# Attention block with 32 experts on one core: earlier bias selectors, a later change of slots, other places for raw rows and gates

## The chip, the core and the metric

The kernel runs on one core of a Trainium2 chip. TensorE (PE) multiplies, VectorE (DVE) and ScalarE (ACT) work on the results and prepare operands, GpSimd (POOL) and SyncE (SP) issue most of the loads. The metric is the device time of one execution in microseconds; before the change the median of three runs is 1178.18 us (1177.84 to 1178.41).

## The reference

One layer for 256 tokens of width 1024, all in fp32. A projection `w_in` feeds three attention branches (fox with a forget gate, dilated, and attention to a memory) and three gates. The branches are merged and projected, and a layer norm follows. A router picks 4 of 32 experts for each token, and a last layer norm ends the layer.

```python
merged = (gates[:, :, 0] * jnp.einsum('bse,ed->bsd', o_fox, w_br_fox[l])
          + gates[:, :, 1] * jnp.einsum('bse,ed->bsd', o_dil, w_br_dil[l])
          + gates[:, :, 2] * jnp.einsum('bse,ed->bsd', o_mem, w_br_mem[l]))
y = jnp.einsum('bsd,de->bse', merged, w_out[l])
h = layer_norm(DEEPNORM_ALPHA * h + y, ln1_g[l], ln1_b[l])
y_moe = moe_ffn(h.reshape(B * S, D), w_router[l], b_router[l], w_exp_in[l], b_exp_in[l], ...)
h = layer_norm(DEEPNORM_ALPHA * h + y_moe, ln2_g[l], ln2_b[l])
...
def expert_block(args):                      # in moe_ffn
    xe, e = args
    h = xe @ w1[e] + b1[e]
    return clamped_swiglu(h) @ w2[e] + b2[e]
```

The weights of one expert are a 1024 x 2048 and a 1024 x 1024 matrix, 12.58 MB; all 32 make 402 MB.

## The kernel before

**Attention.** Weights arrive in pieces. Each lands in one of four raw slots (w0 to w3), ACT casts it (`L212`, the high part), DVE subtracts the cast from the raw form (`L205`, the low part), and PE forms three products of high and low parts (`L225`, `product`). The split views lie in a ring of slots h4 to h7 and h2. `use()` runs before each step of PE and splits some steps ahead. The transposed tokens (`xT`) and the memory (`memT`) are the first operands; before the change their pieces go through the same four raw slots. `load_to(n)` issues a piece's DMA on SP. The matrices come in the order g0, kv, mq, fv, fq, fk, dq, dk, dv, g2, g4, br0, g1, g3, g5, br1, wo (g: gates, br: branch projections, wo: output projection).

**Rows of the biases.** `raw1` holds the rows of b1, `raw2` those of b2 and of the norms. `rows_of` (L641 to L649) splits them into high and low parts b1s, b2s and lnr. Before the change POOL loads them at the start, and they are split between the steps of the gates g1 and g3.

**Norm stage.** The output projection, the residual, the layer norm, router and top 4 are interleaved by hand (L790 to L862).

**Experts.** Each expert handles up to 64 tokens. `gather` picks its tokens with a product by a one-hot matrix, `inner` is the first matrix product (bias product L938, weights L945), `swiglu` follows, `outer` is the second product (L977, L983), and `scatter` (L993) adds to the accumulators. The order on PE is inner(e + 1), outer(e), gather, scatter(e). In experts 1 to 4 a `residual` adds a piece of the residual as well. The bias product multiplies b1s by `own`, a matrix that selects the rows of expert e; `choose(e)` makes it on DVE:

```python
own[e] = p2.tile([P, P], F32R, tag="own", name="own")
nc.vector.tensor_scalar_mul(own[e], c2[:, CBL:CUS], c2[:, CSUM + e:CSUM + e + 1])
```

**Order of the weight stream.** `unit` (L903 to L924) loads 2 MB of expert weights into the next of eleven small places of 16 KB a partition (`turn`; some consist of two half slots, each with its own DMA). From expert LARGE on it loads 4 MB into five places of 32 KB a partition (`turn2`), which lie over the small ones: a big slot can be loaded once the small units under it have been used. A place is loaded again when the products that read it have ended. SP issues in its written order, and a DMA whose place isn't free holds all behind it. The first eleven units are put among the attention's weight pieces (`issue_after`, EXPERTS_FROM).

PE, DVE and ACT run in the order in which the code is written (`manual_schedule`); SP and POOL are ordered by a scheduler.

Of the kernel before, what the change touches and what calls it, by code (L numbers as in the profile page):

```python
# [11 lines left out]
F32 = mybir.dt.float32  # L12
# [9 lines left out]
P = 128  # L22
# [6 lines left out]
C = 64  # L29
# [12 lines left out]
LARGE = 10  # L42
# [39 lines left out]
def block_kernel(ctx: ExitStack, tc: tile.TileContext, x, xT, memT, w_in, b_fgate, t5, w_mem_kv, w_br, w_out,  # L82
# [10 lines left out]
    EXPERTS = ("H01", "h4", "h5", "H67", "X", "O", "W", "h2", "h3", "M", "m", "e", "E")  # L93
# [34 lines left out]
    s = const.tile([P, 2, GB, C], F32, name="s")  # L128

# [10 lines left out]
    with ExitStack() as s1:  # L140
# [22 lines left out]
        plan, views, raw, marks, steps, n_load, n_part, n_ring, n_used = [], [], [], [], [], [0], [0, 0], [0], [0]  # L163
# [6 lines left out]
        def x_piece(src, v, k, n):  # L170
            plan.append((src[:, k:k + n], lambda: v[k // 4][:, :, k % 4:k % 4 + n]))

        def w_piece(src, where, k, n):

            i, f = len(plan), src.shape[-1]
# [11 lines left out]
            plan.append((src[:, k:k + n], take))  # L187
# [4 lines left out]
        def load_to(n):  # L192
            while n_load[0] < min(n, len(plan)):
                src = plan[n_load[0]][0]
                k, f = src.shape[1:]
                raw.append(slot(f"w{n_load[0] % 4}", k, f))
                marks.append(nc.sync.dma_start(raw[-1], src))
                n_load[0] += 1

        def split(a, b):  # L200

            while n_part[0] < a or n_part[1] < b:
                if n_part[1] < min(b, n_part[0]):
# [3 lines left out]
                    load_to(i + 5)  # L207
                else:
                    i = n_part[0]
                    load_to(i + 1)  # L210
# [17 lines left out]
        def cols(i, n=P):  # L228
            return slice(i * n, (i + 1) * n)
# [40 lines left out]
        mT, mv_ = halves("o")  # L270
        W = {}
# [20 lines left out]
        matrix("wo", w_out, n=1)  # L292

# [187 lines left out]
        nc.tensor.matmul(po[:, P:T], lf[1], NU[:, 0:P], start=False, stop=True)  # L481
        g = turned(xTs, W["fk"], 3, "ps_k")
        next(g)
        ckf = at.tile([P, T], F32, tag="o", name="ckf")
# [3 lines left out]
        next(g)  # L488

# [3 lines left out]
        next(g)  # L493
        ps = next(g)
        k_f = evict_qk(ps, 3, False, "k_f")

# [98 lines left out]
        gate2 = pg.tile([P, 4, T], F32, tag="gt2", name="gt2", bufs=1)  # L595
# [4 lines left out]
        pz = s6.enter_context(tc.tile_pool(name="pz", bufs=4, space=PSUM, **TILES))  # L600
# [11 lines left out]
        zeros = p3.tile([P, 512], BF16, name="zeros", bufs=1)  # L612
# [16 lines left out]

        raw1, raw2 = place(0, F32, "raw1"), place(1, F32, "raw2")  # L630
        nc.gpsimd.memset(raw2, 0.0)
        for g in range(2):
            for i in range(2):
                r = slice(64 * g + 32 * i, 64 * g + 32 * i + NE)
                nc.gpsimd.dma_start(raw1[r].rearrange("p (i f) -> p i f", i=2),
                                    b1.rearrange("e (i g f) -> e g i f", i=2, g=2)[:, g])
                nc.gpsimd.dma_start(raw2[r, 0:512], b2[:, cols(g, 512)])
        for i in range(2):
            nc.gpsimd.dma_start(raw2[32 * i:32 * i + 8, 512:1024], ln.rearrange("r (g f) -> (r g) f", g=2))

        def rows_of(i):  # L641

            src, dst, n = ((raw1, b1s.rearrange("p i f -> p (i f)"), 2), (raw2[:, 0:512], b2s, 2), (raw2[0:C, 512:1024], lnr, 1))[i // 2]
            if i % 2 == 0:
                nc.scalar.copy(dst, src)
            else:
                for g in range(n):
                    r = slice(64 * g + 32, 64 * g + 64)
                    nc.vector.tensor_sub(dst[r], src[r], dst[r].bitcast(F32))  # L649

        mg_t = []
        mgT = lambda u, k: mg_t[k // 4][:, u, k % 4].bitcast(F32R)
        for c in range(2):
            gates = [gate01[:, 0:4], gate01[:, 4:8], gate2] if c == 0 else []
            for b in range(len(gates), 3):
                for i, ps in enumerate(turned(xTs, W[f"g{2 * b + c}"], 4, "ps_g", new=bank2)):
                    if b < 2 and i % 2 == 0 or b == 1 and i % 2:
                        rows_of(i // 2 if b == 0 else 2 + i)
                g = pg.tile([P, 4, T], F32, tag=f"gt{b}", name=f"gt{b}", bufs=1) if b else slot("h3", 4, T)
# [21 lines left out]
        s6.close()  # L681
# [90 lines left out]
        def ahead(n):  # L772

            for i in range(n):
                nc.tensor.matmul(gx[i % 2], zeros[:, 0:P], zeros, start=True, stop=False)
# [13 lines left out]

        nc.scalar.activation(zT[0][:, 0, 0:1], mg_t[1][:, 0, 3, T - 1:T], AF.Sqrt, scale=0.0)  # L790
# [16 lines left out]
        normal(0, 0, nc.scalar)  # L807
        choice(0)
# [10 lines left out]
        normal(0, 1, nc.scalar)  # L819
        ahead(2)  # L820
        route(1, range(4, 6))
        turn_back(1, 6, 2)
# [49 lines left out]
    with ExitStack() as s1:  # L872
# [25 lines left out]
        turn = (("N",), ("H01",), ("h2", "e"), ("E",), ("X",), ("O",), ("W",), ("M",), ("h3", "h4"), ("H67",), ("h5", "m"))  # L898
# [4 lines left out]
        def unit(e, u, large, pieces=1, last=False):  # L903
# [14 lines left out]
            for c in [0, 2048, 4096, 6144, 7168] if last else range(0, w * len(names), n):  # L918
# [3 lines left out]
                with tc.issue_after(before.ins) if n_u[0] <= len(turn) else ExitStack():  # L922
                    loads.append(nc.sync.dma_start(at(c, n), src))
            return at  # L924

        own, own_last = {}, []

        def choose(e):

            own[e] = p2.tile([P, P], F32R, tag="own", name="own")  # L930
            nc.vector.tensor_scalar_mul(own[e], c2[:, CBL:CUS], c2[:, CSUM + e:CSUM + e + 1])  # L931
# [99 lines left out]
        with tc.manual_schedule(engines={PE, DVE, ACT}):  # L1031

            choose(0)
# [267 lines left out]
```

## Time and profile before

| | |
|---|---|
| median of 3 runs | 1178.18 us |
| profiled execution | 1178.88 us |
| its span | 1176.7 us |
| PE busy | 1104.2 us (94%) |
| DVE, ACT busy | 330.3 us (28%), 208.6 us (18%) |
| bytes moved | 443.90 MB, mean 377 GB/s |
| SP's queue | 36576 packets, 440.15 MB, 90.4% of 16 engines' span |

The span runs from the first to the last instruction on the core; the execution's time is 2.2 us longer. The busy share of PE is an average: it counts products that run at the slow clock, and products that only follow the arrival of weights. Which of the two, PE or the weight stream, is late at a place is read from the waits there. "Clock" is the granted clock of PE as a share of the full one (1.00 is 2.4 GHz, 0.50 is 1.2 GHz).

### The profile page before, as it was taken

The page shows a single profiled execution, that of the slowest core. Times are in us where ns is not written, and L with a number is a line of the kernel's source. Part 1 is how long each engine was busy: PE and PEld are TensorE (multiplying, and loading weights), DVE is VectorE, ACT ScalarE, POOL GpSimd, SP SyncE. Part 2 cuts the span into 40 slices and gives each one's busy share as a digit, 9 for nine tenths or more (in the row PEclk, how much of TensorE's full clock was granted, in tenths as well). Part 3 has the DMA queues.
Part 4 walks back from the last instruction along what each step waited for, and adds up shares of the span by engine and source line. Part 5 has one row for each costly group of instructions (what it writes and reads, how often), then busy time and mean ns, then how long its engine had stood idle before and what let it go on. Part 6 is the DMA issues. An engine that isn't in the chain of part 4 may idle for free.

```text
span 1176.7 us, 13733 instructions
## 1 busy us (share of the span) xinstructions
PE 1104.2 (94%) x5854; PEld 543.5 (46%) x5854; DVE 330.3 (28%) x662; ACT 208.6 (18%) x391; POOL 17.4 (1%) x36
## 2 busy tenths in 40 slices
PE   7999999979999999999999999999999998999996
PEld 6899899734333333333333333333333333333322
DVE  4656675622221212111111221111111111111113
ACT  4655544421000001000100100000000000000011
POOL 3000110000000000000000000000000000000000
PEclk8999999989999999999999999999999999999999
DMA  7964687879999999879999999999999999999992
GB/s 229 314 216 148 221 283 239 325 316 428 424 427 427 425 423 422 361 321 431 435 431 429 429 433 433 432 427 432 433 431 429 432 433 429 431 428 427 425 421 115
DMA packets 37745, 443.90 MB, mean 377 GB/s; under 512 B 4442, under 2 KB 4736, under 8 KB 17712
## 3 DMA queue, kind: packets, MB, share of 16 engines
q1 hardware_dynamic: 36576, 440.15, 90.4%
q0 software_dynamic: 1104, 2.82, 1.0%
q8 instruction: 48, 0.79, 0.3%
q14 instruction: 17, 0.14, 0.0%
HBM read 441.90 MB, written 1.06 MB: 376 GB/s over the span
## 4 chain that ended last, share of the span: by engine, by line
PE 49%; DMA 30%; DVE 5%; ACT 2%; issue 1%; DVEq 0%; ACTq 0%
PE h L945 22%; PE yp L983 13%; DMA slot_DC<-in_wx 11%; DMA slot_DB<-in_wx 7%; DMA slot_DD<-in_wx 6%; DMA slot_DA<-in_wx 3%; PE ps_x L886 3%; DMA slot_DF<-in_wx 3%; PE ps_g L225 2%; PE h L938 1%; PE ps_b L225 1%; PE y L225 1%; ACT xe L891 1%; PE ps_a L969 1%; DVE xe L893 1%; PE acc L993 1%
## 5 line engine op out<-in xcount | busy, mean ns | idle before, releaser
L1249 DVE TENSOR_SCALAR h<-h 128x512 f32<-128x512 f32 x32 | 22.4, 699 | 438.3 <-PE h L945 438.3
L962 ACT COPY sgT<-ps_s 128x256 f32<-128x256 f32 x32 | 11.9, 372 | 498.1 <-PE ps_s L960 498.1
L205 DVE TENSOR_TENSOR slot_h<-slot_w,slot_h 128x1024 fp32r<-128x1024 f32 (+3 forms) x73 | 78.5, 1089 | 33.5 <-ACT slot_h L212 33.2
L225 PE MATMUL ps_g<-slot_x,slot_h 128*128 128x256 f32 x576 | 74.4, 291 | 5.7 <-ACT slot_h L212 3.7
L212 ACT CAST slot_h<-slot_w 128x1024 fp32r<-128x1024 f32 (+3 forms) x73 | 68.1, 944 | 49.0 <-PE ps_g L225 8.8
L225 PEld LDWEIGHTS ps_g<-slot_x,slot_h 128*128 128x128 f32 x576 | 72.4, 198 | 7.8 <-ACT slot_h L212 4.8
L986 DVE COPY ys<-yp 128x512 f32<-128x512 f32 x31 | 21.4, 692 | 184.1 <-PE yp L983 184.1
L945 PE MATMUL h<-slot_DF,xe 128*64 128x512 f32 x288 | 63.9, 595 | 1.8 <-DMA slot_DF<-in_wx 1.8
L971 ACT COPY actT<-ps_a 128x512 f32<-128x512 f32 x32 | 18.7, 585 | 260.6 <-PE ps_a L969 260.6
L945 PE MATMUL h<-slot_DD,xe 128*64 128x512 f32 x288 | 63.6, 594 | 0.0
L945 PE MATMUL h<-slot_DC,xe 128*64 128x512 f32 x288 | 63.6, 594 | 0.0
L945 PE MATMUL h<-slot_DB,xe 128*64 128x512 f32 x288 | 63.5, 593 | 0.0
L993 PE MATMUL acc<-ys,sgT 64*128 64x512 f32 x248 | 61.6, 615 | 0.4 <-DVE ys L986 0.4
L886 PE MATMUL ps_x<-s,zn 128*128 128x128 f32 x480 | 58.3, 275 | 0.0
L945 PE MATMUL h<-slot_DA,xe 128*64 128x512 f32 x256 | 56.6, 594 | 0.1
L886 PEld LDWEIGHTS ps_x<-s,zn 128*128 128x128 f32 x480 | 55.9, 192 | 0.0
L893 DVE TENSOR_SCALAR xe<-ps_x,lnc 128x128 f32<-128x128 f32 x60 | 24.6, 410 | 79.0 <-ACT xe L891 79.0
L938 PE MATMUL h<-b1s,own 128*128 128x512 f32 x64 | 23.7, 453 | 23.4 <-DVE own L931 23.4
L983 PE MATMUL yp<-slot_DA,actT 128*64 128x512 f32 x160 | 37.4, 619 | 4.2 <-DMA slot_DA<-in_wx 4.2
L983 PE MATMUL yp<-slot_DC,actT 128*64 128x512 f32 x160 | 35.9, 597 | 5.4 <-DMA slot_DC<-in_wx 5.4
L945 PEld LDWEIGHTS h<-slot_DF,xe 128*64 128x64 f32 x288 | 20.1, 137 | 42.9 <-issue 38.0
L983 PE MATMUL yp<-slot_DD,actT 128*64 128x512 f32 x128 | 33.4, 683 | 6.0 <-DMA slot_DD<-in_wx 6.0
(316 smaller groups left out, 1260.2 us busy)
## 6 DMA issues: line engine op xcount, KB each, us to landing
slot_DC<-in_wx SPq DMA_DIRECT2D x12, 4096.0 KB, 38.5
slot_DB<-in_wx SPq DMA_DIRECT2D x12, 4096.0 KB, 39.2
slot_DA<-in_wx SPq DMA_DIRECT2D x11, 4096.0 KB, 38.8
slot_DD<-in_wx SPq DMA_DIRECT2D x11, 4096.0 KB, 38.5
slot_DF<-in_wx SPq DMA_DIRECT2D x11, 4096.0 KB, 39.4
slot_h<-in_wx SPq DMA_DIRECT2D x21, 1024.0 KB, 13.6
slot_H<-in_wx SPq DMA_DIRECT2D x10, 2048.0 KB, 13.9
slot_w<-in_w_in_g SPq DMA_DIRECT2D x23, 512.0 KB, 4.8
```

Source lines behind the costliest of these rows:

```text
L205: nc.vector.tensor_sub(views[i][:, 1].bitcast(F32R), raw[i], views[i][:, 0])
L212: nc.scalar.copy(views[i][:, 0].bitcast(F32R), raw[i])
L225: nc.tensor.matmul(ps, a(u, k)[:, ca], b(v, k)[:, cb], start=first and i + j == 0, stop=last and i == 2 and j == len(ks) - 1)
L886: nc.tensor.matmul(ps[:, i * GB * C:(i + 1) * GB * C], zn[tt][:, (c + i) * P:(c + i + 1) * P], s[:, tt].rearrange("p a b -> p (a b)"), sta ...
L893: nc.vector.tensor_scalar(t[:, c + i, :], ps[:, i * GB * C:(i + 1) * GB * C], g, b_, op0=ALU.mult, op1=ALU.add)
L938: nc.tensor.matmul(hp[i], own[e], b1s[:, i], start=True, stop=False)
L945: nc.tensor.matmul(hp[i][g * C:(g + 1) * C, :], xt[:, k, s0:s0 + C], wt(k % n * 2 * FF + i * FF + g * 512, 512), start=False, stop=k == KD ...
L971: nc.scalar.copy(actT, ps.rearrange("p (a b) -> p a b", a=4))
L983: nc.tensor.matmul(yp[g * C:(g + 1) * C, :], actT(k), wt(k % n * D + g * 512, 512), start=False, stop=k == KD - 1)
L986: nc.vector.tensor_copy(ys, yp)
L993: nc.tensor.matmul(acc[tt][g], sgT[r, tt * P:(tt + 1) * P], ys[r, :], start=e == 0, stop=False)
L1249: nc.vector.tensor_scalar_min(hg, hg, LIMIT)
```

## The change

- `choose` moves to the constants with three buffers. It makes the selectors of experts 0 and 1 before the norm stage, that of 2 in expert 0, and afterwards each one an expert ahead, behind `swiglu`.
- LARGE goes from 10 to 12: 70 small units instead of 58, then 61 big ones.
- The raw form of the tokens and the memory has a slot of its own (N), and `load` counts only the weight pieces against the four raw slots.
- The raw rows of biases and norms are loaded by SP behind a weight piece of the middle of the attention, and split among the fk products.
- The gates gt1 and gt2 lie in the buffers of `xe`, gt0 in the place of zn0; gates and branch products stay in the banks of pool `pp`, which closes later.
- (h3, f) is the fifth place of the turn, and the order and the layout of the small places are new. E is the fourth in both.
- In the norm stage `normal(0, 1)`, `turn_back(1, 6, 2)` and `route(1, range(4, 6))` stand earlier, and the fillers of `ahead` read a smaller operand.

```diff
-LARGE = 10
+LARGE = 12
...
-    EXPERTS = ("H01", "h4", "h5", "H67", "X", "O", "W", "h2", "h3", "M", "m", "e", "E")
+    EXPERTS = ("H01", "h4", "h5", "H67", "X", "O", "W", "h2", "h3", "a", "b", "f", "e", "E")
...
+    def choose(e):
+        own[e] = const.tile([P, P], F32R, tag="own", name="own", bufs=3)
+        nc.vector.tensor_scalar_mul(own[e], c2[:, CBL:CUS], c2[:, CSUM + e:CSUM + e + 1])
...
         def x_piece(src, v, k, n):
-            plan.append((src[:, k:k + n], lambda: v[k // 4][:, :, k % 4:k % 4 + n]))
+            r = xraw[:, (0 if v is xv else KD) + k:][:, 0:n]
+            plan.append((src[:, k:k + n], lambda: v[k // 4][:, :, k % 4:k % 4 + n], r))
...
+        def load():
+            while n_load[0] < len(plan):
+                src, _, r = plan[n_load[0]]
+                if r is None:
+                    if n_load[1] - sum(p[2] is None for p in plan[:n_part[1]]) == 4:
+                        return
+                    r = slot(f"w{n_load[1] % 4}", *src.shape[1:])
...
+        with tc.issue_after(marks[30].ins):
+            for i in range(2):
+                nc.sync.dma_start(raw2[32 * i:32 * i + 8, 512:1024], ln.rearrange("r (g f) -> (r g) f", g=2))
+                for g in range(2):
...
+        rows_of(0)
         g = turned(xTs, W["fk"], 3, "ps_k")
         next(g)
+        rows_of(1, (0,))
...
         next(g)
+        rows_of(1, (1,))
+        rows_of(2)
...
         next(g)
+        rows_of(3)
+        rows_of(4)
         ps = next(g)
         k_f = evict_qk(ps, 3, False, "k_f")
+        rows_of(5, (0,))
...
-        s5.close()
         py = s3.enter_context(tc.tile_pool(name="py", bufs=1, space=PSUM, side="right", **TILES))
...
-                ps = [bank2("ps_b") for i in range(2)]
+                ps = [bank("ps_b") for i in range(2)]
...
+        for i in range(2):
+            choose(i)
...
-        turn = (("N",), ("H01",), ("h2", "e"), ("E",), ("X",), ("O",), ("W",), ("M",), ("h3", "h4"), ("H67",), ("h5", "m"))
+        turn = (("N",), ("H01",), ("h2", "e"), ("E",), ("h3", "f"), ("X",), ("O",), ("h4", "a"), ("W",), ("H67",), ("h5", "b"))
...
-            choose(0)
             hp = inner(0)
             sg = placed(0)
-            choose(1)
             act = swiglu(nc, p2, *hp)
...
             act = swiglu(nc, p2, *hp)
+            choose(2)
             ys = outer(0, actT, "h0")
...
-                choose(e + 1)
                 sg = placed(e)
...
                 act = swiglu(nc, p2, *hp)
+                if e < NE - 2:
+                    choose(e + 2)
```

On DVE among the fk products, up to the copy of k_f, the order before is this (slot_h from slot_w is the low part of a weight piece):

```order
L205 TENSOR_TENSOR slot_h_816<-slot_w_713,slot_h_816 128x768
L491 CAST eye<-c_63 128x128
L492 CAST eye<-cs 128x128
L205 TENSOR_TENSOR slot_h_847<-slot_w_753,slot_h_847 128x768
L205 TENSOR_TENSOR slot_h_873<-slot_w_783,slot_h_873 128x768
L265 COPY k_f<-ps_k 128x512
L265 COPY k_f<-ps_k 128x256
L205 TENSOR_TENSOR slot_h_896<-slot_w_814,slot_h_896 128x768
```

And after:

```order
L217 TENSOR_TENSOR slot_h_822<-slot_w_705,slot_h_822 128x768
L515 TENSOR_TENSOR b1s<-raw_803,b1s 32x1024
L530 CAST eye<-c_63 128x128
L531 CAST eye<-cs 128x128
L217 TENSOR_TENSOR slot_h_854<-slot_w_745,slot_h_854 128x768
L515 TENSOR_TENSOR b2s<-raw_804,b2s 32x512 x2
L217 TENSOR_TENSOR slot_h_882<-slot_w_775,slot_h_882 128x768
L276 COPY k_f<-ps_k 128x512
L276 COPY k_f<-ps_k 128x256
L515 TENSOR_TENSOR lnr<-raw_804,lnr 32x512
L217 TENSOR_TENSOR slot_h_908<-slot_w_820,slot_h_908 128x768
```

The split of b1's second half and of b2 stands ahead of the copy of k_f; b1's first half stands seven rows ahead of the first row shown.

On SP, around unit 3 and 4 of the experts (slot_e, slot_E), before:

```order
L923 DMA slot_e<-in_wx 128x2048
L197 DMA slot_w_1754<-in_w_in_g 128x1024
L197 DMA slot_w_1783<-in_w_in_g 128x1024
L923 DMA slot_E<-in_wx 128x4096
L197 DMA slot_w_1816<-in_w_in_g 128x1024
L197 DMA slot_w_1851<-in_w_in_g 128x1024
L197 DMA slot_w_1890<-in_w_in_g 128x1024
L197 DMA slot_w_1920<-in_w_in_g 128x1024
L197 DMA slot_w_1949<-in_w_in_g 128x1024
```

After:

```order
L943 DMA slot_e<-in_wx 128x2048
L943 DMA slot_E<-in_wx 128x4096
L209 DMA slot_w_1750<-in_w_in_g 128x1024
L209 DMA slot_w_1779<-in_w_in_g 128x1024
L209 DMA slot_w_1812<-in_w_in_g 128x1024
L209 DMA slot_w_1847<-in_w_in_g 128x1024
L943 DMA slot_h_2851<-in_wx 128x2048
L943 DMA slot_f<-in_wx 128x2048
L209 DMA slot_w_1886<-in_w_in_g 128x1024
L209 DMA slot_w_1915<-in_w_in_g 128x1024
```

E is directly behind e, ahead of two gate pieces that were ahead of it, and (h3, f) has come in among the next ones.

On DVE at the change from the norm stage to the experts (gov is the last of the router's rows, sg and h are of expert 0), before:

```order
L862 SCALAR_TENSOR_TENSOR gov<-posx,gate 128x64
L931 TENSOR_SCALAR own<-c_63 128x128
L953 TENSOR_SCALAR sg<-c_63,posx,gate 128x128 x2
L931 TENSOR_SCALAR own<-c_63 128x128
L1249 TENSOR_SCALAR h_2792<-h_2792 128x512
L1250 TENSOR_SCALAR sw_l<-h_2793 128x512
```

After:

```order
L882 SCALAR_TENSOR_TENSOR gov<-posx,gate 128x64
L968 TENSOR_SCALAR sg<-c_63,posx,gate 128x128 x2
L1264 TENSOR_SCALAR h_2785<-h_2785 128x512
L1265 TENSOR_SCALAR sw_l<-h_2786 128x512
L1267 SCALAR_TENSOR_TENSOR sw_l<-sw_l,h_2785 128x512
```

The selectors of expert 0 and 1 are gone from here. In their new place they stand on DVE ahead of the first residual:

```order
L217 TENSOR_TENSOR slot_h_2455<-slot_w_2393,slot_h_2455 128x1024
L217 TENSOR_TENSOR slot_h_2473<-slot_w_2413,slot_h_2473 128x1024
L134 TENSOR_SCALAR own<-c_63 128x128 x2
L742 SCALAR_TENSOR_TENSOR xs<-xs,y_2387 128x512
L813 BN_STATS st_2491<-xs 128x6
```

They follow the last low parts of the output projection's weights.

## Rows read from the trace of the kernel before

**Rows 1.** the page's first line

```profile
span 1176.7 us, 13733 instructions
```

**Rows 2.** the chain that ended last; start us, us, engine and tile

```profile
667.98 36.79 DMA slot_DC<-in_wx
...
1146.15 1.96 PE yp L983 x8
```

**Rows 3.** stretches; us, busy and (x) of PE, PEld, DVE, ACT, POOL, clock, DMA, GB/s

```profile
12.00:18.00 6.00, 5.49 (x25) 5.45 (x26) 2.62 (x4) 2.11 (x3) 0.00 (x0) 0.50 1.01 281
244.00:252.00 8.00, 6.63 (x20) 2.26 (x22) 1.92 (x13) 1.30 (x2) 0.00 (x0) 0.60 0.27 111
320.00:360.00 40.00, 36.90 (x159) 13.87 (x161) 8.09 (x17) 2.36 (x5) 0.00 (x0) 0.91 1.01 426
470.00:500.00 30.00, 29.28 (x141) 11.38 (x143) 5.76 (x14) 2.40 (x5) 0.00 (x0) 1.00 0.88 364
500.00:530.00 30.00, 29.37 (x145) 11.32 (x143) 5.32 (x11) 2.40 (x5) 0.00 (x0) 1.00 0.79 321
600.00:700.00 100.00, 97.86 (x481) 38.42 (x479) 17.84 (x38) 8.68 (x18) 0.00 (x0) 1.00 1.00 431
```

**Rows 4.** timeline of all engines, 239 to 253 us; start us, us, instruction, idle before

```profile
245.37 1.22 PE L938 MATMUL h<-b1s,own 128*128 128x512 f32 x2 [4.98 <-DVE own L931]
...
246.52 5.56 PE L945 MATMUL h<-slot_N,xe 128*64 128x512 f32 x16
...
252.12 0.33 SPq L923 DMA_DIRECT2D slot_N<-in_wx  x1
```

**Rows 5.** timeline of PE, 8 to 30 us

```profile
11.25 0.63 PE L225 MATMUL ps_g<-slot_x,slot_h 128*128 128x256 f32 x2 [2.84 <-ACT slot_h L212]
12.51 11.24 PE L225 MATMUL ps_g<-slot_x,slot_h 128*128 128x256 f32 x70 [0.63 <-DVE slot_h L205]
```

**Rows 6.** timeline of DVE, 155 to 182 us

```profile
166.73 2.47 DVE L649 TENSOR_TENSOR b1s<-raw,b1s 32x1024 fp32r<-32x1024 f32 x2
...
173.32 1.40 DVE L649 TENSOR_TENSOR b2s<-raw,b2s 32x512 fp32r<-32x512 f32 x2
```

**Rows 7.** timeline of all engines, 66.5 to 82 us

```profile
68.28 3.02 SPq L197 DMA_DIRECT2D slot_w<-in_w_in_dq  x2
...
70.61 0.83 ACT L212 CAST slot_h<-slot_w 128x768 fp32r<-128x768 f32 x1
...
77.40 1.14 DVE L265 COPY k_f<-ps_k 128x512 f32<-128x512 f32 x2 [1.23 <-PE ps_k L225]
...
80.17 0.93 PE L349 MATMUL sc_f<-k_f,q_f 64*128 64x128 f32 x8
```

**Rows 8.** DMA issues, 0 to 20 us; KB each, us to landing

```profile
raw<-in_b POOLq DMA_DIRECT2D x4, 128.0 KB, 7.3
```

**Rows 9.** timeline of PE, 134 to 170 us

```profile
145.54 11.78 PE L225 MATMUL ps_b<-slot_o,slot_h 128*128 128x256 f32 x96 [1.95 <-ACT gt L304]
```

**Rows 10.** DMA issues, 140 to 165 us

```profile
slot_w<-in_w_in_g SPq DMA_DIRECT2D x6, 512.0 KB, 6.5
slot_E<-in_wx SPq DMA_DIRECT2D x1, 2048.0 KB, 13.2
```

**Rows 11.** DMA issues of the whole span, from the page

```profile
slot_w<-in_w_in_g SPq DMA_DIRECT2D x23, 512.0 KB, 4.8
```

**Rows 12.** waits; us in total, times, longest

```profile
PE h L938 <- DVE own L931: 23.4, 29, 5.0
```

**Rows 13.** the chain again, experts 4 to 9

```profile
353.71 15.14 PE h L945 x64
...
384.82 13.88 PE h L945 x64
...
470.42 0.70 PE h L938 x2
...
497.22 0.70 PE h L938 x2
```

More of the change, by code (lines that the diff above doesn't have):

```diff
@@ L162, in block_kernel @@
         RING, LATE = (4, 5, 6, 7, 2), 40
-        plan, views, raw, marks, steps, n_load, n_part, n_ring, n_used = [], [], [], [], [], [0], [0, 0], [0], [0]
+        plan, views, raw, marks, steps, n_load, n_part, n_ring, n_used = [], [], [], [], [], [0, 0], [0, 0], [0], [0]
         def halves(i):
@@ L186, in take @@
                 return t[:, :, a:a + n]
-            plan.append((src[:, k:k + n], take))
+            plan.append((src[:, k:k + n], take, None))
         def part(where):
             return lambda u, k: where[k][0][:, u, where[k][1]].bitcast(F32R)
[L192 to L197, printed above, removed]
+        def load():
[5 more added lines that the diff above has]
+                    r = slot(f"w{n_load[1] % 4}", *src.shape[1:])
+                    n_load[1] += 1
+                raw.append(r)
+                marks.append(nc.sync.dma_start(r, src))
                 n_load[0] += 1
@@ L270, in block_kernel @@
         mT, mv_ = halves("o")
+        xraw = slot("N", 2 * KD, T)
         W = {}
@@ L292, in block_kernel @@
         matrix("wo", w_out, n=1)
+        load()
         warm = at.tile([P, 512], BF16, name="warm", bufs=1)
@@ L627, in block_kernel @@
         nc.gpsimd.memset(zero, 0.0)
[L630 to L649, printed above, removed]
         mg_t = []
@@ L655, in block_kernel @@
             for b in range(len(gates), 3):
[L656 to L659, printed above, removed]
+                for ps in turned(xTs, W[f"g{2 * b + c}"], 4, "ps_g"):
+                    pass
+                g = px.tile([P, 4, T], F32, tag="xe", name=f"gt{b}") if b else place(0, F32, "gt0").rearrange("p (a t) -> p a t", a=4)
                 sigmoids(ps, g)
@@ L774, in ahead @@
             for i in range(n):
-                nc.tensor.matmul(gx[i % 2], zeros[:, 0:P], zeros, start=True, stop=False)
+                nc.tensor.matmul(gx[i % 2].rearrange("p (a b) -> p a b", a=4), zeros, zeros[:, None, :].to_broadcast([P, 4, P]),
+                                 start=True, stop=False)
         def gather0(tt, ks):
@@ L818, in block_kernel @@
         nc.vector.bn_stats(st[1][:, 2], xs[:, 1, 768:1024])
[L819 removed]
+        turn_back(1, 6, 2)
+        route(1, range(4, 6))
         ahead(2)
[L821 to L822 removed]
         variance(1)
@@ L921, in unit @@
                 before = marks[EXPERTS_FROM + 8 * (n_u[0] - 1) + 2 * (c // n)] if early else loads[-1]
-                with tc.issue_after(before.ins) if n_u[0] <= len(turn) else ExitStack():
+                with tc.issue_after(before.ins) if n_u[0] <= len(turn) else ExitStack(), tc.high_priority() if n_u[0] <= len(turn) else ExitStack():
                     loads.append(nc.sync.dma_start(at(c, n), src))
             return at
[L926 to L931, printed above, removed]
+        own_last = []
         def inner(e, tags=("h0", "h1")):
@@ L1091, in last_norm @@
         def last_norm(pool, z, st, last):
-            ts = slot("M", 5, 512)
+            ts = slot("X", 5, 512)
             ta = ts[:, 4:5]
@@ L1174, in block_kernel @@
             nc.vector.memset(one1, 1.0)
-            hT = slot("H01", KD, T)
+            hT = slot("h4", KD, T)
             for tt in range(2):
@@ L1182, in block_kernel @@
             with tc.For_i(0, NE, 1) as e:
-                wt = [slot(i, 1, 4096)[:, 0] for i in ("X", "O", "W", "H67", "E", "M")]
+                wt = [slot(i, 1, 4096)[:, 0] for i in ("H01", "H67", "X", "O", "W", "E")]
                 for u in range(6):
```

28 lines of the change are left out of this document (21 added, 7 removed).

## Prediction

> **What bounds the kernel now.** The times below are those of the one profiled execution: its span is 1176.7 us [rows 1], its program time 1178.88 us, 2.2 us more; the median of the runs shown is 1178.18 us, 0.7 us less. A span that I work out is therefore raised by 1.5 us to stand beside the median.
>
> I read the chain of waits first, from its end backwards. From 668 us on nearly all of it is a DMA of a big expert slot, until the last products at 1146 us [rows 2]; from 668 us there are ten such DMA steps. So the weight stream ends the kernel and PE only follows. Next I read the table of stretches for where that stream isn't full [rows 3]. Between 600 and 700 us it has a share of 1.00 at 431 GB/s, and at 320 to 360 us, with the small slots, 1.01 at 426 GB/s. It is short in two places: around 244 to 252 us (0.27), and at the change from small to big slots (364 GB/s in 470 to 500, 321 GB/s in 500 to 530). In the first, all eleven small units have landed and SP waits for PE to give back the first: the issue of unit 12, into N, stands at 252.12 us [rows 4]. In the second, a big slot lies over several small ones and its load waits until PE has used the last of them. A gain therefore counts if it brings the issue at 252 us forward, or if it fills the hole at the change of slots. A gain of PE elsewhere is worth only what it does to these two.
>
> **Up to the issue at 252 us.** Here PE is the path, and the change touches it in five places.
>
> The first operands get their raw form apart, so their loads no longer turn in four slots with the weights and SP issues the first eight without a wait. Before, PE stops for 2.84 and 0.63 us at 11.25 and 12.51 us [rows 5], the longer one on an ACT cast that had to have its piece. From 12 to 18 us it then runs at a granted clock of 0.50, the 1.2 GHz level: 25 products take 5.49 us, 0.22 each [rows 3], while the other 45 of the 70 [rows 5] take 11.24 - 5.49 = 5.75 us, 0.128 each. Half clock costs 25 x 0.092 = 2.3 us. At most all of 2.84 + 0.63 + 2.3 = 5.8 us goes; at least nothing, if the queue itself is the limit. The pieces were held back by their place in the order alone, so I take -4.5, near the full end.
>
> The rows of the biases and of the norm are split into high and low part at the fk products instead of the gates. Before k_f is copied, DVE gets b1s twice and b2s twice: 2.47 + 1.40 us by their rows at their old place [rows 6], 3.9 in all. DVE had 1.23 us to spare there, its wait for ps_k ahead of the copy at 77.40 us; the copy ended at 78.54, and PE took sc_f only at 80.17 [rows 7], so 1.6 us of slack follow. Without more, PE would be 3.9 - 1.2 - 1.6 = 1.1 us late. ACT also casts b1s between the eviction of q_f and the next dq weights, whose cast began at 70.61 us [rows 7], and it waits for its raw rows. These loads now stand on SP behind the dq piece issued at 68.28 us [rows 7]; on POOL such a load took 7.3 us beside others [rows 8]. Landed at 68.28 + 7.3 = 75.6 they would hold ACT by 5.0 us, landed at once by nothing. The link is half empty there, so I take 2, near the lower end: 3.1 for the stall. Behind a stop of this size at the start came half clock for 2.3 us (above), so I add 1.7, the stop being shorter on most sides. Together +4.8, between 0 (slack behind it takes it up) and 1.1 + 5.0 + 2.3 = 8.4. Behind the cast on ACT stand the casts of the dq weights, behind the subs on DVE their low parts and k_f; PE waits for both.
>
> The Trainium skill (TensorE: Matmul & The Clock Gate, Part 1: The HAM clock gate) calls the slow clock the array's default, which only activity lifts. The trace agrees with 0.50 after the stop at 11.25 us, and this speaks against the change here: without it the term is 3.1, by it 4.8.
>
> The gates and branch products stay in the old pool of banks, so ps_b at 145.54 us loses its wait of 1.95 us for the sigmoids [rows 9]. Against that, unit E now goes out right behind e, ahead of g1's third piece. A gate piece took 6.5 us in 140 to 165 us, where e and E pass, and 4.8 us as the median of 23 [rows 10, 11]: +1.7 for the pieces that meet 2 MB more. Sum -0.2, between -1.95 and -1.95 + 4.9 (2.1 MB at 426 GB/s) = +2.9. Unit (h3, f) now goes among g3's pieces; the weights there have slack of their kind, so I take +0.5, between 0 and 1.7. The Trainium skill (DMA: Bandwidth & Descriptors, Queues, rings and completion order) has each engine take a queue's transfers in ring order. By that a piece behind E is late by the whole 4.9 us and the sum would be 3 us worse; E's own 13.2 us, where 4.9 would do alone [rows 10], shows that transfers in flight share, and I keep to the rows.
>
> The norm stage's new order moves two products of row 1 ahead of two fillers and one normalisation up: no engine gets more work, 0, and no more than 0.5 either way.
>
> The selection of expert 0's biases is made before the norm stage. Before, PE stood 4.98 us at 245.37 for `own` (L931), which DVE reaches only behind the gates' softmax [rows 4]. The changed bias product waits for nothing of DVE, and the gathered tokens that the next products need are evicted as they were, one after another, each before its turn. That is -5.0, all of it. With the idle time goes the half clock behind it: L938 took 1.22 us for two and slot_N's 16 products 5.56 us [rows 4], where 64 take 13.88 us at full clock [rows 13], 3.47 for 16; the two of L938 take 0.70 elsewhere. 2.09 + 0.52 = -2.6.
>
> Sum: -4.5 + 4.8 - 0.2 + 0.5 + 0 - 5.0 - 2.6 = -7.0. The one more early unit buys nothing in itself, as all eleven have landed before 244 us in both. I let the issue at 252 us move by -13 to -1.
>
> **The change of slots.** The missing bytes in 470 to 530 us are 30 x (1 - 364/431) = 4.7 and 30 x (1 - 321/431) = 7.7 us [rows 3], 12.4 in all. This is how far PE came too late for DC, and then for DB and DA. What does PE gain on the stream before the change now? The waits for `own` are 23.4 us over 29 [rows 12]; without the first, 18.4, of which the experts before the change hold about 10 (1.6 to 2.0 in each of the four with a residual). Three of these waits drop the clock: 64 products take 15.14 instead of 13.88 us [rows 13], 3 x 1.26 = 3.8. Two experts more before the change: PE needs 497.22 - 470.42 = 26.8 us for one [rows 13], the stream 12.58 MB / 431 = 29.2, so 2 x 2.4 = 4.8. Together 18.6, more than 12.4. The new turn asks DC to wait for the unit seven back instead of eight (some 4.5 us tighter, a sixth of 26.8), DB eight instead of seven and DA seven instead of six (looser by as much). DC alone was 4.7 late: 4.7 + 4.5 = 9.2, still below 18.6. So the hole closes: -12.4, between -8 and -12.4. What is late next is nothing: the stream is full.
>
> **Later.** Twelve more units, 25.2 MB, go at 426 instead of 431 GB/s: 25.2/0.426 - 25.2/0.431 = +0.7, from 0 to 1.5. The own waits after the change cost nothing, PE has 2.4 us an expert in hand there. The tail behind the last load is as before.
>
> **Sum.** 1176.7 - 7.0 - 12.4 + 0.7 = 1158.0 span, 1160.2 program, 1159.5 beside the median. I forecast 1160 us; its own range is 1155 to 1165.
>
> **Rivals.**
> A, better: the rows land in time at fk and the start gives all its 5.8. Then the issue at 252 us moves by -11 to -13: 1154 to 1156. For it: the fk pieces leave SP idle at times. Against: 3.9 us more DVE work are sure.
> B, the hole at the change of slots stays in good part, because `own` was only the last of several to come and another wait (the residual's rows, a bank) takes its place in experts 1 to 4. Then PE gains 8.6 of 18.6, DC is still 0.5 late and what lies behind it adds to it; with 6 to 12 us left, 1166 to 1172. For it: DVE does two residual rows just ahead of `own`. Against: the bias product doesn't read them.
> C, what is saved before 252 us is given back: fk at +8.4 and E at +2.9 make -4.5 + 8.4 + 2.9 + 0.5 - 5.0 - 2.6 = -0.3 in place of -7.0: 1167. For it: rows of this kind took 7.3 us to land [rows 8]. Against: the gates' stage has weights in hand.
> D, slower: the weights of the attention starve behind expert units. N's pieces, E and (h3, f) are all before pieces that PE needs; if PE waits each in full, 3 x 4.9 = 14.7, and each such stop is followed by half clock as at the start, 3 x 2.3 = 6.9, together 21.6: 1160 + 21.6 = 1182. It decides from 18.5 us on, where every gain is used up. For it: SP is one queue. Against: gate pieces beside E took 1.7 us more, not 4.9 [rows 10, 11].
> E, the gains come to nothing in the sum by parts of B, C and D: 1178.
>
> **Chances.** Forecast 0.51, A 0.15, B 0.13, C 0.14, D 0.04, E 0.03. Two runs of this kernel can't be told apart within 0.2%, some 2.4 us. Faster is the forecast with A, B and C, 0.93; same 0.03; slower 0.04. The range takes in A, C and the most of B: 1152 to 1170, leaving out D, E, the far end of B and a little on the low side.
>
> **What would show it.** Right: the first issue into N near 245 us; no wait of expert 0's bias product for `own`; the two stretches around the change of slots (now near 585 us) at 426 GB/s or more; the last load landing some 19 us earlier. The step on fk is wrong if PE's product sc_f comes without a stop, that on the start if PE still stops at 8 to 12 us. The whole is wrong if the stream pauses in 560 to 630 us, or if the issue into N isn't before 250 us.

## The result, and the profile after

The changed kernel takes 1168.13 us (median of 5 runs, 1167.02 to 1170.76), the kernel before 1178.18 (1176.23 to 1180.44): a ratio of 0.9916, 95% interval 0.9897 to 0.9934. It is faster by some 10 us, and not by the 18 that I took as likeliest. The profiled execution has a span of 1166.4 us, 10.3 less than before.

The table of stretches of the kernel after, with the columns of [rows 3]; the change of slots now lies between 530 and 590 us:

```profile
12.00:18.00 6.00, 3.59 (x17) 3.39 (x17) 4.36 (x6) 4.37 (x6) 0.00 (x0) 0.75 0.99 362
244.00:252.00 8.00, 6.95 (x50) 4.62 (x50) 3.87 (x18) 4.21 (x8) 0.00 (x0) 1.00 0.86 365
320.00:360.00 40.00, 40.00 (x191) 15.14 (x191) 8.10 (x17) 2.36 (x5) 0.00 (x0) 1.00 1.01 425
530.00:560.00 30.00, 29.98 (x151) 12.02 (x148) 5.67 (x11) 2.77 (x6) 0.00 (x0) 1.00 1.02 434
560.00:590.00 30.00, 29.97 (x150) 12.33 (x150) 6.39 (x15) 3.52 (x8) 0.00 (x0) 1.00 1.00 429
600.00:700.00 100.00, 90.88 (x436) 34.64 (x434) 18.59 (x37) 10.23 (x21) 0.00 (x0) 1.00 1.00 431
```

The hole at the change of slots is gone: shares of 1.02 and 1.00, where [rows 3] had 0.88 and 0.79. The clock stays at 1.00 where the experts with a residual had 0.91. And PE is busy for less between 600 and 700 us (90.88 instead of 97.86 us): it has caught up with the stream and waits for it. The chain of waits shows the same: the first big slot in it stands at 597.59 us, where before it was 667.98 [rows 2], and the last load lands at 1135.8 instead of 1146.1 us. Between 244 and 252 us the link is busy too (0.86 instead of 0.27): the last early unit went out at 240.36 us, 8.6 later than before, and took 12.0 us to land. So the prediction's sentence that all eleven had landed before 244 us doesn't hold for the kernel after.

```profile
597.59 38.66 DMA slot_DD<-in_wx
...
1115.95 19.86 DMA slot_DF<-in_wx
1135.85 1.96 PE yp L998 x8
```

Next the start of the experts, where the first place comes free (timeline of all engines):

```profile
248.73 0.71 PE L953 MATMUL h<-b1s,own 128*128 128x512 f32 x2
...
249.37 3.65 PE L960 MATMUL h<-slot_N,xe 128*64 128x512 f32 x16
...
253.06 0.33 SPq L943 DMA_DIRECT2D slot_N<-in_wx  x1
```

PE no longer waits ahead of the bias product (4.98 us in [rows 4]), and slot_N's products run at full clock, 3.65 instead of 5.56 us. Yet the issue into N comes at 253.06 us, 0.94 later than before. So all that was gained up to here was lost on the way. Two places where PE stops show where. The first is at the fk products (ACT, then PE):

```profile
72.39 1.05 ACT L511 CAST b1s<-raw 128x1024 fp32r<-128x1024 f32 x1 [4.03 <-DMA raw<-in_b]
```

```profile
78.08 2.18 PE L236 MATMUL ps_q<-slot_x,slot_h 128*128 128x256 f32 x16 [0.62 <-DVE slot_h L217]
83.60 1.65 PE L362 MATMUL sc_f<-k_f,q_f 64*128 64x128 f32 x8 [3.34 <-DVE k_f L276]
```

ACT stands 4.03 us for the raw rows, and PE then 0.62 and 3.34 us. The second is at g1 (ACT, PE, then the DMA issues from 140 to 170 us with KB and time to landing):

```profile
165.10 1.05 ACT L223 CAST slot_h<-slot_w 128x1024 fp32r<-128x1024 f32 x1 [9.63 <-DMA slot_w<-in_w_in_g]
```

```profile
148.37 11.77 PE L236 MATMUL ps_b<-slot_o,slot_h 128*128 128x256 f32 x96
159.98 5.92 PE L236 MATMUL ps_g<-slot_x,slot_h 128*128 128x256 f32 x48
166.20 0.50 PE L236 MATMUL ps_g<-slot_x,slot_h 128*128 128x256 f32 x2 [0.30 <-ACT slot_h L223]
171.28 4.00 PE L236 MATMUL ps_g<-slot_x,slot_h 128*128 128x256 f32 x17 [4.59 <-DVE slot_h L217]
```

```profile
slot_w<-in_w_in_g SPq DMA_DIRECT2D x6, 512.0 KB, 9.5
slot_E<-in_wx SPq DMA_DIRECT2D x1, 2048.0 KB, 15.7
```

ps_b has lost its wait of 1.95 us [rows 9]. But ACT waits 9.63 us for the third piece of g1, which stands behind E. E takes 15.7 us, and gate pieces 9.5 us as a median, instead of 6.5 [rows 10]. PE stops for 4.59 us, and the first 17 products after that take 4.00 us, 0.24 each: half clock again (granted clock 0.50 from 171 to 175 us).

### The profile page after: what moved, and what is told of

Same layout as the page of the kernel before. It is cut to its first block, busy times and chain, and to the rows that moved or that the text cites. A ratio compares the mean times of both kernels' runs of the same rounds, so it can differ in the third digit from the quotient of the medians.

```text
span 1166.4 us, 13729 instructions
## 1 busy us (share of the span) xinstructions
PE 1102.1 (94%) x5854; PEld 544.3 (47%) x5854; DVE 331.5 (28%) x662; ACT 208.4 (18%) x391; POOL 12.9 (1%) x26
## 4 chain that ended last, share of the span: by engine, by line
PE 57%; DMA 37%; DVE 3%; ACT 1%; issue 1%; SPq 0%; DVEq 0%; ACTq 0%
PE h L960 20%; PE yp L998 12%; DMA slot_DF<-in_wx 12%; DMA slot_DC<-in_wx 7%; DMA slot_DD<-in_wx 7%; DMA slot_DA<-in_wx 6%; PE ps_g L236 6%; DMA slot_DB<-in_wx 3%; PE acc L1008 3%; PE ps_x L906 3%; DMA slot_w<-in_w_in_g 2%; PE ps_v L236 2%; PE ps_q L236 1%; PE y L236 1%; PE h L953 1%; PE ps_k L236 1%
## 5 line engine op out<-in xcount | busy, mean ns | idle before, releaser
L236 PE MATMUL ps_g<-slot_x,slot_h 128*128 128x256 f32 x576 | 77.1, 296 | 10.1 <-DVE slot_h L217 5.6
L960 PE MATMUL h<-slot_DD,xe 128*64 128x512 f32 x256 | 56.8, 595 | 2.1 <-DMA slot_DD<-in_wx 2.1
L960 PE MATMUL h<-slot_DB,xe 128*64 128x512 f32 x256 | 56.6, 595 | 1.1 <-DMA slot_DB<-in_wx 1.1
L960 PE MATMUL h<-slot_DC,xe 128*64 128x512 f32 x256 | 56.7, 595 | 0.8 <-DMA slot_DC<-in_wx 0.8
L960 PE MATMUL h<-slot_DF,xe 128*64 128x512 f32 x256 | 56.5, 594 | 0.0
L998 PE MATMUL yp<-slot_DB,actT 128*64 128x512 f32 x128 | 32.0, 655 | 8.0 <-DMA slot_DB<-in_wx 8.0
L998 PE MATMUL yp<-slot_DA,actT 128*64 128x512 f32 x128 | 33.4, 682 | 6.1 <-DMA slot_DA<-in_wx 6.1
L911 ACT ACTIVATE xe<-ps_x,lnc 128x128 f32<-128x128 f32 x60 | 27.4, 457 | 48.2 <-PE ps_x L906 33.9
L960 PEld LDWEIGHTS h<-slot_DD,xe 128*64 128x64 f32 x256 | 17.8, 137 | 38.6 <-issue 34.0
L960 PEld LDWEIGHTS h<-slot_DA,xe 128*64 128x64 f32 x256 | 17.9, 137 | 38.4 <-issue 34.6
```

The costliest lines, as they stand in the source:

```text
L236: nc.tensor.matmul(ps, a(u, k)[:, ca], b(v, k)[:, cb], start=first and i + j == 0, stop=last and i == 2 and j == len(ks) - 1)
L911: nc.scalar.activation(t[:, c + i, :], ps[:, i * GB * C:(i + 1) * GB * C], AF.Identity, scale=g, bias=b_)
L960: nc.tensor.matmul(hp[i][g * C:(g + 1) * C, :], xt[:, k, s0:s0 + C], wt(k % n * 2 * FF + i * FF + g * 512, 512), start=False, stop=k == KD ...
L998: nc.tensor.matmul(yp[g * C:(g + 1) * C, :], actT(k), wt(k % n * D + g * 512, 512), start=False, stop=k == KD - 1)
```

## Experiments

Two numbers split each run. The issue into N tells what the first 250 us do. The span less that issue tells what the stream does afterwards; it doesn't feel the scatter of the first stage, which is large (last section). Times are medians, while the last two columns come from each kernel's one profiled execution and carry its scatter; ratios are against the kernel before on the same chip, whose median there was 1179.64 or, for the last three kernels, 1179.71 us.

| kernel | us | ratio (95%) | issue into N | span less it |
|---|---|---|---|---|
| before | 1178.18 | | 252.12 | 924.6 |
| changed | 1168.13 | 0.9916 (0.9897 to 0.9934) | 253.06 | 913.3 |
| E behind g1's weights | 1162.11 | 0.9861 (0.9844 to 0.9879) | 246.28 | 913.2 |
| rows split at the gates | 1160.52 | 0.9836 (0.9820 to 0.9851) | 248.19 | 912.6 |
| both of these | 1154.96 | 0.9805 (0.9789 to 0.9821) | 240.38 | 912.7 |
| raw rows in a block | 1161.54 | 0.9852 (0.9835 to 0.9868) | 246.08 | 913.2 |
| selectors late | 1170.11 | 0.9930 (0.9912 to 0.9948) | 250.63 | 915.0 |
| selectors in p2 | 1180.75 | 1.0004 (0.9990 to 1.0019) | 260.48 | 915.5 |
| LARGE 10 | 1171.47 | 0.9924 (0.9900 to 0.9948) | 254.84 | 915.3 |
| LARGE 10, selectors late | 1185.67 | 1.0059 (1.0041 to 1.0078) | 250.38 | 930.4 |
| both, operands in the ring | 1161.18 | 0.9851 (0.9836 to 0.9866) | 245.74 | 913.4 |
| both, (h3, f) later | 1156.50 | 0.9803 (0.9789 to 0.9816) | 241.30 | 913.3 |
| raw rows in a block, E later | 1157.47 | 0.9814 (0.9800 to 0.9827) | 245.22 | 913.3 |

**E behind g1's weights.**

```diff
-                before = marks[...] if early else loads[-1]
+                before = marks[...] if early else marks[61] if n_u[0] == 4 and not large else loads[-1]
```

> The changed kernel with one edit: unit E goes out behind the fourth piece of g1 instead of ahead of the third. Theory W (two waits of PE cost the start its gain: 5.7 us at the fk products and 4.9 us of stop plus 1.8 us of half clock at g1, and both pass whole to the first issue into N at 253.1 us and to the end): the stop of 4.59 us ahead of ps_g falls to 1.2 us or less, the issue into N comes at 246 to 248 us, the time is 1162. Rival Q (SP's queue has the same bytes to bring before 250 us, so what one piece gains the next loses, here at g3 behind E and (h3, f)): the issue into N comes at 250 us or later, the time is 1165 or more.

Measured: 1162.11 us, the issue into N at 246.28. The timeline of PE:

```profile
166.38 8.78 PE L236 MATMUL ps_g<-slot_x,slot_h 128*128 128x256 f32 x71 [1.86 <-DVE slot_h L217]
```

A stop of 1.86 us is left, more than I said (the last experiment shows what makes it). Otherwise it is as theory W has it: by the medians the 2 MB ahead of the weights cost the change 6 us. Within the trace, where E acts, from the first product of one branch projection (ps_b) to that of the next, it is 5.1 us (53.38 to 48.29); the rest of the 6.8 us at the issue into N is scatter of the stages before (mq starts at 33.25 instead of 36.42 us, the fk stage is 1.5 us longer).

**Rows split at the gates.**

```diff
-        rows_of(0)
         g = turned(xTs, W["fk"], 3, "ps_k")
...
+                    if b < 2 and i % 2 == 0 or b == 1 and i % 2:
+                        j = i // 2 if b == 0 else 2 + i
+                        rows_of(j, (0,) if j == 5 else (0, 1))
```

> The changed kernel with one edit: the rows of biases and norms are split at g1 and g3 as before the change; their loads stay on SP. Theory W: no stop ahead of sc_f, the issue into N at 247 to 248 us, the time 1162 to 1163. Rival Q: DVE and ACT have the same work to do at g1 and g3, where E has already made the weights late, so the stop there grows by 3 us or more; the issue into N at 250 us or later, the time 1166.

Measured: 1160.52 us, the issue into N at 248.19, and sc_f without a stop. The same work at the gates costs next to nothing there: from one ps_b to the next it takes 53.20 us, in the changed kernel 53.38. That it is hidden because PE waits for the weights there anyway is how I read it.

```profile
80.35 0.93 PE L362 MATMUL sc_f<-k_f,q_f 64*128 64x128 f32 x8
```

**Both edits together.**

> The changed kernel with both edits: E behind the fourth piece of g1, and the rows split at g1 and g3. Theory W: the gains add, the issue into N comes at 240 to 242 us, the time is 1156 to 1157. Rival Q: the issue into N at 246 us or later, the time 1162 or more. A third outcome: N is issued at 241 us, but the stream still brings the last early units then, and less than the whole of it reaches the end.

Measured: 1154.96 us, the issue into N at 240.38. The gains add (13.2 us by the medians, 6.0 and 7.6 alone), and both pass to the end in full (the span less the issue is 912.7, after the change 913.3). This is the fastest version, faster than both kernels; its timeline:

```profile
240.38 0.33 SPq L938 DMA_DIRECT2D slot_N<-in_wx  x1
```

**Raw rows in a block.** This separates the two things that I had put into the term at fk, the landing and the added DVE work. (The clearing of raw2 on POOL, ahead of these loads, gets the same priority.)

```diff
-        with tc.issue_after(marks[30].ins):
+        with tc.issue_after(marks[30].ins), tc.high_priority():
```

> The changed kernel with one edit: all raw rows of biases and norms are issued in a block behind the first fk piece (48 to 54 us in the changed kernel's trace) and not spread up to 70 us; they are still split among the fk products. Theory R (the stop ahead of sc_f comes from the landing: ACT stood 4.03 us at the cast of b1s and everything behind it was late): no wait of that cast, the stop ahead of sc_f at most 0.5 us, the time 1162 to 1163. Rival V (the 3.9 us more DVE work ahead of the copy of k_f make it): the stop stays at 2.5 us or more, the time 1167 or more. A third outcome: 0.8 MB ahead of the fk weights make those late, with a new stop of 1 to 3 us before 70 us.

Measured: 1161.54 us. The cast of b1s comes without a wait and so does sc_f (ACT, then PE):

```profile
67.68 1.05 ACT L512 CAST b1s<-raw 128x1024 fp32r<-128x1024 f32 x1
```

```profile
78.88 0.93 PE L362 MATMUL sc_f<-k_f,q_f 64*128 64x128 f32 x8
```

The landing makes the stop. The 3.9 us of DVE work alone nearly fit in: from the first fk product to the second group of sc_f it takes 17.17 us, before the change 16.79.

**Raw rows in a block, and E later.** The two edits above as one.

> The changed kernel with the raw rows in a block behind the first fk piece (split among the fk products as in the change) and E behind g1's fourth piece. Theory W (the two waits are apart from each other): the time is that of both edits, 1155 to 1156, with the issue into N at 239 to 242 us. Rival Q: 1158 or more, since the block of rows and E meet the same weights.

Measured: 1157.47 us, between the two expectations. The trace has a slow start, a stop of 3.01 us at 13.5 us; that execution was also the slowest of the five. That the two waits are apart from each other is borne out only roughly.

**Selectors late.**

```diff
-        for i in range(2):
-            choose(i)
...
+            choose(0)
             hp = inner(0)
             sg = placed(0)
+            choose(1)
...
+                choose(e + 1)
                 sg = placed(e)
...
-                if e < NE - 2:
-                    choose(e + 2)
```

> The changed kernel with one edit: the selectors are made where they were before the change (the first one behind gov, each other one at the head of its expert). Theory L (the hole at the change of slots closed because PE caught up with the stream by what it no longer waits for the selectors, 10 us and 3.8 us of half clock, and 4.8 us from two more experts): the issue into N 7.5 us later at 260.6, and of the hole of 12.4 us some 7.6 come back, 1183 in all. Rival S (two more experts and the new places of the slots close it by themselves): the issue into N at 260.6, no hole, 1175.6.

Measured: 1170.11 us, and neither theory. There is no wait ahead of expert 0, and of the hole only a trace is there (timeline of PE, then the stretch with the columns of [rows 3]):

```profile
246.30 0.71 PE L951 MATMUL h<-b1s,own 128*128 128x512 f32 x2
```

```profile
530.00:560.00 30.00, 29.70 (x147) 11.42 (x145) 4.98 (x10) 2.40 (x5) 0.00 (x0) 1.00 0.99 412
```

On DVE the selector of expert 0 still stood far ahead, though the code makes it at the first expert:

```profile
27.06 0.28 DVE L134 TENSOR_SCALAR own<-c 128x128 fp32r<-128x128 f32 x1
```

That of expert 1 came at 251.61 us, behind gov. So the order of the code on DVE does not hold across the stages as I had described it, and what I expected of the next kernel, that the first two were still early, is true of the first alone. This kernel undid only the later selectors.

**Selectors in p2.** As selectors late, with the tile back in the pool of the expert stage.

```diff
-        own[e] = const.tile([P, P], F32R, tag="own", name="own", bufs=3)
+        own[e] = own_pool[0].tile([P, P], F32R, tag="own", name="own")
```

> The changed kernel with the selectors back in the expert stage's pool p2 and at their old places in the code. With the selectors late but in the constants the first product waited for nothing, since the first two were still made early. Theory M (the wait of 4.98 us before expert 0 came from the memory of p2, which is free only when the router's rows are done, and not from the place in the code): the wait is back with 5 us and with it the half clock, the issue into N at 258 to 260 us, the span less the issue into N 915 as with late selectors, the time 1176 to 1177. Rival T (something else in the new order removes that wait): the issue into N at 251 to 253 us, the time 1170.

Measured: 1180.75 us, the whole gain gone. The wait is back, with the half clock (timeline of PE):

```profile
254.53 1.22 PE L952 MATMUL h<-b1s,own 128*128 128x512 f32 x2 [4.99 <-DVE own L134]
255.68 4.76 PE L959 MATMUL h<-slot_N,xe 128*64 128x512 f32 x16
```

The code has the selector at the same place in this kernel and the one above; they differ in the pool alone. So the pool makes the wait, by keeping the selector from moving ahead on DVE. That p2's memory is free only behind the router's rows is how I read it; on DVE `own` stands right behind gov in this kernel (254.19 us).

**LARGE 10.**

```diff
-LARGE = 12
+LARGE = 10
```

> The changed kernel with one edit: LARGE is 10 again, the change of slots comes after 58 small units. The span less the issue into N (924.6 us before, 913.3 after, 915.0 with the selectors made late) tells the hole without the noise of the first 250 us. Theory L (PE's gain by the selectors and the clock, 13.8 us, covers the hole of 12.4 alone): 913 to 915, the time 1168. Rival S (two more experts, 4.8 us, are what closes it): 917 to 921, the time 1173 to 1176. Rival P (the new places of the slots close it whatever PE does): 912 to 913, since twelve units fewer go at the lower rate of the small slots.

Measured: 1171.47 us, 915.3 us behind the issue. The stretch at the change of slots, now at 470 us, lacks 30 x (1 - 394/431) = 2.6 us:

```profile
470.00:500.00 30.00, 29.98 (x148) 11.24 (x144) 5.69 (x11) 2.40 (x5) 0.00 (x0) 1.00 0.95 394
```

Theory L is near: PE's gain alone nearly covers the hole.

**LARGE 10, selectors late.** Both edits above.

> The changed kernel with LARGE at 10 and the selectors made late, from expert 2 on at the head of their expert. Theory L: neither gain of PE is there, the hole is back with 8 to 10 us, the span less the issue into N is 921 to 923, the time 1176 to 1178. Rival P (the new places of the slots close it): 913 to 915, the time 1168.

Measured: 1185.67 us, 930.4 us behind the issue, 17 more than the changed kernel and 6 more than before the change. SP's issues and the stretch:

```profile
472.58 0.33 SPq L941 DMA_DIRECT2D slot_e<-in_wx  x1
499.39 0.33 SPq L941 DMA_DIRECT2D slot_DC<-in_wx  x1
```

```profile
470.00:500.00 30.00, 29.70 (x145) 11.32 (x143) 4.99 (x10) 2.40 (x5) 0.00 (x0) 1.00 0.48 200
```

With LARGE at 10 the new turn lets DC wait for the unit six back (52 of 58), where it was eight before and is seven with LARGE at 12 (63 of 70). The hole is larger than before the change, so rival P falls, and theory L, which had 921 to 923 behind the issue, is too small. That this place of DC makes it so large is read from the code. Either alone, the early selectors or LARGE at 12, brings the hole down to some 2 us: they aren't a sum, each nearly suffices. What LARGE at 12 does is two things at once, two more experts and DC's place in the turn, and no run splits them.

**Both, operands in the ring.** The kernel with both edits, and the tokens' and memory's pieces in the four raw slots again.

```diff
-            r = xraw[:, (0 if v is xv else KD) + k:][:, 0:n]
-            plan.append((src[:, k:k + n], lambda: v[k // 4][:, :, k % 4:k % 4 + n], r))
+            plan.append((src[:, k:k + n], lambda: v[k // 4][:, :, k % 4:k % 4 + n], None))
```

> The kernel with both edits (E behind g1's fourth piece, rows split at g1 and g3) and in addition the first operands' pieces back in the four raw slots of the weights, as before the change. The first ps_q of mq began at 37.04 us before the change and at 36.42, 33.25, 37.47, 34.60 and 33.55 us in five traces with the pieces apart. Theory X (apart they are worth 2 us in the mean, and what is left of the loss is the queue itself): that product begins at 36.5 to 37.5 us, the issue into N at 242 to 244 us, the time is 1157. Rival O (they are worth nothing, the spread is chance): 33 to 37 us as apart, the time 1155.

Measured: 1161.18 us, 6 more than with the pieces apart. But the first product of mq comes at 34.62 us, as with the pieces apart (34.60 in the trace with both edits). The loss is later (timeline of PE, then ACT):

```profile
45.27 2.08 PE L360 MATMUL sc_m<-k_m,q_m 64*128 64x256 f32 x8 [2.59 <-ACT q_m L273]
```

```profile
43.88 0.84 ACT L222 CAST slot_h<-slot_w 128x780 fp32r<-128x780 f32 x1 [2.56 <-DMA slot_w<-in_w_in_fv]
```

ACT evicts q_m late because it waits for the weights of fv ahead of it, whose first piece SP issues at 31.41 instead of 26.50 us. Up to the fk products this costs 3.6 us; another 1.7 are lost at the gates, again with half clock. So the pieces apart are worth some 5 us in this surrounding (one trace of each, 6 us by the medians), and neither theory had the place: not at the first products, but in the lead that the later weights get.

**Both, (h3, f) later.**

```diff
+                before = ... marks[{4: 61, 5: 65}[n_u[0]]] if n_u[0] in (4, 5) and not large and c == 0 else loads[-1]
```

> The kernel with both edits and in addition unit (h3, f) behind the fourth piece of g3 instead of ahead of the third. Theory H (the stop of 1.86 us that is left in the gates, at 160.5 us in the trace with both edits, comes from E and (h3, f) ahead of g3's weights): the stop is under 0.6 us, the issue into N 1 to 2 us earlier than 240.4, the time 1153 to 1154. Rival E (the stop is made by E alone, ahead of g3's first pieces): it stays at 1.5 to 2 us, the time 1155.

Measured: 1156.50 us; the stop is as it was (timeline of PE), so (h3, f) doesn't make it:

```profile
161.36 3.86 PE L236 MATMUL ps_g<-slot_x,slot_h 128*128 128x256 f32 x30 [1.86 <-DVE slot_h L217]
```

Nor does E, as rival E has it. Between 147 and 161 us ACT waits for PE and DVE, never for a load, and the low part that PE waits for stands on DVE right behind the merging of the branch product (mg):

```profile
159.48 0.69 DVE L690 TENSOR_TENSOR mg<-slot_h,mg 128x512 fp32r<-128x512 f32 x1 [0.69 <-ACT mg L689]
160.09 3.49 DVE L217 TENSOR_TENSOR slot_h<-slot_w,slot_h 128x1024 fp32r<-128x1024 f32 x3
```

The stop is the same 1.86 us in the traces with E behind g1's weights and with both edits; before the change it was 1.16.

## Why the prediction was right or wrong

The direction was right, and the hole at the change of slots closed. The other part of the gain did not come: the issue into N, which I let move by -13 to -1 us, moved by +0.9. Of the cases it was rival C that came, the one with 0.14 (1167 us): all that is saved before 252 us is given back. The time lies inside the stated range because that range took in C, not because the sum behind 1160 us held, and one of the signs that I gave for the whole being wrong, an issue into N that isn't before 250 us, did come. The last load lands 10.3 us earlier, not some 19. The bounds of the terms, added up, even reach from -15.9 to +5.9; -13 to -1 was narrower than they allow. Term by term, from the trace after:

| term | forecast | measured |
|---|---|---|
| first operands apart, up to the fk products | -4.5 | -0.9 (69.21 to 68.35) |
| rows split at fk | +4.8 | +5.7 (81.51 - 69.21 = 12.30 to 86.08 - 68.35 = 17.73, and 0.3 up to 90.84) |
| ps_b without its wait | -1.95 | -2.0 |
| E ahead of g1's weights | +1.7 | +5.8 |
| (h3, f), norm stage | +0.5 | -0.1 |
| selector of expert 0 | -5.0 | -5.1 |
| half clock behind it | -2.6 | -2.4 |
| sum at the issue into N | -7.0 | +0.9 |
| change of slots with the slower small units | -11.7 | -11.3 |

- **The step that failed most** is the one on E: "+1.7 for the pieces that meet 2 MB more". I took the difference of two medians, 6.5 and 4.8 us [rows 10, 11], for the price of standing behind E. But of the six pieces in the first of them three stood ahead of E. The first piece behind E was issued at 152.01 us and cast at 164.36, without a wait for it: it had time. The third piece of g1 now has all of e and E ahead of it and is needed at once: E was issued at 148.03 us and took 15.7, so it landed at 163.7; ACT stood ready from 155.47 us, and the cast came at 165.10. Behind it on ACT and DVE stands the merging of the branch product, and only behind that, at 170.01 us, the low part that PE waits for. The rule of the Trainium skill that I had weighed and left (DMA: Bandwidth & Descriptors, Queues, rings and completion order: each engine takes a queue's transfers in their order) fits this. The bound of +2.9 for the sum of the two ps_b terms, which went by 4.9 us, was too tight as well (measured +3.8), since the stop also brought half clock for 1.8 us. With E put back, the time falls by 6 us, 5.1 of them at this place.
- **The start** failed by nearly as much (-0.9 instead of -4.5). I took the pieces to be held back by their place in the order alone. Now SP issues them early, and they land late: as medians the tokens' pieces take 9.6 us and the gate pieces 9.1 (DMA issues, 0 to 20 us, after), where before it was 5.9 and 5.7. The DMA engines were at 1.00 and 1.01 in 8 to 12 and 12 to 18 us before, and are at 0.98 and 0.99 now. This is the other end that the term named, the queue itself as the limit. PE still stops (DMA issues with KB and time to landing, then the timeline of PE):

```profile
slot_w<-in_w_in_g SPq DMA_DIRECT2D x3, 512.0 KB, 9.1
slot_N<-in_xT SPq DMA_DIRECT2D x3, 256.0 KB, 9.6
```

```profile
8.97 0.51 PE L236 MATMUL ps_g<-slot_x,slot_h 128*128 128x256 f32 x2 [0.70 <-ACT slot_h L223]
13.65 0.50 PE L236 MATMUL ps_g<-slot_x,slot_h 128*128 128x256 f32 x2 [2.49 <-ACT slot_h L223]
```

  A single trace cannot size the term. In eleven traces with the operands apart the first product of mq comes at 33.25 to 37.47 us, 35.4 in the mean, against 37.04 in the one trace before. With the ring back it was 34.62. What the edit gives, by the run with the ring, is a lead for later weights, which I hadn't on the list.
- **fk** was right in its mechanism (the cast waits for its raw rows, what is queued behind it is late, then half clock) and 0.9 us too small in this trace; in the six traces in which the rows are loaded and split as in the change the term runs from 5.3 to 9.0. The split of the term was not quite right: I gave 1.1 us to DVE's work, and with the raw rows in a block the stage is only 0.4 us longer than before the change.
- **The selector** was right in both sizes. That its pool and not its place does it I hadn't seen.
- **The change of slots** closed as forecast. My account of 18.6 us as a sum of three gains was too simple: with the later selectors back the hole is some 2 us instead of 7, and with LARGE at 10 as well it is some 17 (930.4 - 913.3). What a place of the turn is worth (DC at six, seven or eight units back) depends on LARGE modulo the turn, and I had left that aside.

The forecast took the good end of two unknowns, the start and E, both from rows of other situations. Rival C had the outcome, though by a larger term at fk and a smaller one at E than came.

## What to carry to other kernels

Before a transfer is moved ahead of others on one queue, take its whole duration at the stream's rate as the price for the first piece that comes to stand behind it and is needed soon (here an estimate of 4.9 us by the rate; putting E back gave 5.1 us at that place, half clock included); a median of neighbours in the row hides it. Where a long stream ends the kernel, measure an edit at the two points that set it (the first issue that waits, and what lies behind): a gain and a loss ahead of the first cancel without a mark on the total. And where an engine waits for a small operation that needs nothing late, look at the pool that its tile lives in before moving the code.

## What the runs showed that I hadn't expected

The first stage scatters from one execution to the next with the same products: the start of mq by 4.2 us (33.25 to 37.47, both on one chip). Part of it is the clock: the 70 products behind the first operands took 8.65 us in one trace (E behind g1's weights, granted clock 1.00 from 12 to 18 us) and 11.33 in another (rows split at the gates, 0.67). And SP itself can be held at an issue. After eight loads in a row, of which the first two at least had landed (ACT cast them at 3.26 and 4.37 us), the ninth took 3.40 us to issue in the trace after the change, where most take 0.4:

```profile
4.52 3.40 SPq L209 DMA_DIRECT2D slot_N<-in_xT  x1
```

What holds SP there isn't settled by these runs.
